# One transformer layer on one core: one written order for first stage, attention and output projection

## The chip, the cores and the metric

The kernel runs on one core of one Trainium2 chip. The metric is device time in microseconds (us), the median of three runs. A core has TensorE (PE, with its weight loads as PEld), VectorE (DVE), ScalarE (ACT), GpSimd (POOL) and SyncE (SP), which runs the DMA queue of the weights. SBUF is the on-chip memory, PSUM the banks into which TensorE sums.

## The reference

One encoder layer with 256 tokens, width D = 2048, 32 query heads and 8 key/value heads of 64, and an MLP of width 8192. A vector c modulates it: six rows of 2048 values scale, shift and gate.

```python
mod = silu(c) @ mod_w + mod_b                       # 2048 x 12288
sh_m, sc_m, g_m, sh_f, sc_f, g_f = split(mod, 6)
h = x * (1 + sc_m) + sh_m
q, k, v = split(h @ w_qkv + b_qkv)                  # 2048, 512, 512 columns
q, k = rope(q), rope(k)
s = mask(q @ k.T / 8)                               # |q - k| <= 128
p = softmax with a learned sink logit per head (s)
x = layer_norm(alpha * x + (1 + g_m) * ((p @ v) @ w_o + b_o))
h = x * (1 + sc_f) + sh_f
u = square(relu(h @ w1 + b1))
out = layer_norm(alpha * x + (1 + g_f) * (u @ w2 + b2))
```

## The kernel before

**Products.** Tokens come in two tiles of 128. A product in fp32 is done as three products of split numbers (mm3, L684 to L687): high part with high part (L685), high with the low part of the weight (L686), low with high (L687). Weights come in chunks of 1 MB, 128 x 2048 numbers, on the queue of SyncE (L335) into a ring of raw buffers: 5 of them, and 3 more (raws2) in the first stage. ScalarE casts each half of a chunk to its high part wh (L382, L393), VectorE subtracts that from the raw numbers and gets the low part wl (L351). The rings of wh and wl have 5 buffers each. A chunk of the first stage is 24 matmuls with 512 moving columns.

**Modulation.** mod_w is 96 chunks of 1 MB. Each is either taken by TensorE or by VectorE. On TensorE (Mod.quad, L455 to L463) four matmuls with 32 columns each stand side by side in the array; a chunk is 32 recorded matmuls of 128 columns or 16 of 256. On VectorE (Col.step, L498) it is one multiply with sum over 128 x 2048 numbers, with the row silu(c) spread over all partitions in cb. MIXP, FFP and GMP say who takes which: of 16 column tiles for the first scale and shift, 10 go to TensorE (two chunks each), of the gate of the mixer 8 chunks, of the MLP's scale and shift 16; together 44 chunks on TensorE and 52 on VectorE. Before the end of the output projection VectorE takes 28 of its.

**First stage.** x is transposed and modulated tile by tile, and each modulated tile can be multiplied with the columns of w_qkv. "Units" are chunks that hold four (tile, column block) pairs, "quarters" are chunks of four tiles by one column block. A planner, first_order (L80), lists the operations of this stage on the three engines with costs and due times for 17 chunks (SEQ); the code emits them in that order, and keep_in_program_order, through S.pinned (L342), makes each engine keep it.

**Attention and output projection** (scores from 165.1 us on, the last projection matmul at 349.16). A loop over n writes them in steps: scores of 4 heads for one token tile (L922), softmax, transposes of the probabilities (L964), the product with the values (L980), and between them a late chunk of w_qkv or a chunk (c, j) of w_o, where c is a block of 512 output columns and j one of four groups of 8 heads. There the Tile framework sets the order on each engine, with a few added order-only dependencies. The output of chunk (c, j) is summed in SBUF: VectorE adds each part to ys (L1075 for j = 0 with the bias, L1077 for j = 1 and 2). After j = 2, project_0 (L1084) multiplies by the gate and adds alpha times x (L1088, L1089). After j = 3, add_gated (L986) does the gate product, the addition to x and the LayerNorm statistics (L989, L990, L991).

**Behind the projection.** When the last block has its statistics, norm_scalars (L1002) computes mean and inverse deviation on VectorE (with one square root on ScalarE), normed applies them: for the first token tile on VectorE (L1032), for the second on ScalarE (nmr at L1027, applied at L1030). Then TensorE transposes the tile (L1167), ScalarE or VectorE modulates it (L1173, L1179), and the first MLP product with the chunks w1a begins (L1238). At the same time pump (L356) emits casts, low parts and modulation of the chunks that come next; of the MLP's modulation four chunks for TensorE are planned just behind the first chunk of w1a (plan_late(4)), and W1_FILL spreads the rest between the chunks of w1a.

Of the kernel before, what the change touches and what calls it, by code (L numbers as in the profile page):

```python
# [66 lines left out]
SEQ = [(0, [1, 2]), (1, [3]), (2, []), ((0, 3), [4]), ((0, 4), [5]), (3, [6]), (4, [7]), (5, []), ((1, 3), [8]), ((1, 4), [9]), (6, [10]), (7, [11]), (8, [12]), ((2, 3), [13]), (9, [14]), (10, [15]), (11, [])]  # L67
# [3 lines left out]
def first_loads():  # L71

    out = [("m", 0, 0), ("m", 0, 1)]
    for n, ks in SEQ:
        out.append(("w", n))
        out += [("m", k, i) for k in ks for i in range(2)]
    return out


def first_order():  # L80

    cost = dict(gP=1.1, gD=2.37, r=.27, c=.3, a=.16, H=.55, T=.42, S=.42, h=1.0, l=1.18, u=1.37, e=.6, sp=.85, cp=.6)
    ops = {}

    def op(key, eng, after, rank, kind=None):
        ops[key] = eng, cost[kind or key[0]], after, rank

    for k in range(NK):
        g0, g1 = ("g", k, 0), ("g", k, 1)
        if MIXP[k]:  # L90
            op(g0, "PE", [("m", k, 0)], 0, "gP")
            op(g1, "PE", [("m", k, 1), g0], 0, "gP")
            op(("r", k), "ACT", [g1], 0)
            op(("c", k), "PE", [("r", k)], 0)
            op(("a", k), "DVE", [("c", k)], 0)
        else:
            for i, g in enumerate((g0, g1)):
                op(g, "DVE", [("m", k, i), ("cp", 3)], 2, "gD")
# [4 lines left out]

    halves, last, freed = [], {"e": [("cp", 3)]}, []
    for n, _ in SEQ:
        q = type(n) is tuple
        for x in range(2):
            h, l = ("h", n, x), ("l", n, x)
            op(h, "ACT", [("w", n)] + [("h",) + v for v in halves[-1:]], 1)
            op(l, "DVE", [h] + [("l",) + v for v in halves[-1:]], 1)  # L110
# [5 lines left out]
            freed.append(("u", n, 2 + x if q else 2 * x + 1))  # L116
        for i in range(4):
            ks = range(4 * n[0], 4 * n[0] + 4) if q else [UNITS[4 * n + i][0]]
            after = [("l", n, i % 2 if q else i // 2)] + [("S", k) for k in ks] + last.get(q, [])
            if q and i % 2 == 0:  # L120
                after += last.get("e", [])
            op(("u", n, i), "PE", after, 3)
            last[q] = [("u", n, i)]
# [11 lines left out]
    while ops:
        while len(land) < len(loads) and slots:
            v = loads[len(land)]
            d = 2.47 * (1 + XK.get(v[1], 0) / 4 * (v[0] == "m" and v[2] == 0 and v[1] > 0))
            at = max(at, slots.pop(0) + 2.6) + d
            land[v] = at + .1  # L140
        best = None
        for key, (eng, d, after, rank) in ops.items():
            t = engine[eng]
            for x in after:
                if x in done:
                    e, end = done[x]
                    t = max(t, end + (0 if e == eng else .35 if e == "PE" else .15))
                elif x in land:
                    t = max(t, land[x])
                else:  # L150
                    break
            else:
                if best is None or (round(t, 2), rank, ranks[key]) < best[0]:
                    best = (round(t, 2), rank, ranks[key]), key, t
# [1335 lines left out]
```

## Time and profile before

| | |
|---|---|
| three runs | 1086.92, 1085.59, 1086.79 us; median 1086.79 |
| span of the profiled execution | 1083.7 us, 3.1 less than the median |
| last column-tile modulation matmul of the first stage | 132.1 us |
| first and last scores matmul | 165.1, 311.1 us |
| last matmul of the output projection | 349.16 us |
| first matmul of the MLP | 356.10 us |
| modulation chunks on TensorE, on VectorE | 44, 52 |

The profile is that of one execution. The span runs from its first to its last recorded instruction; the time of a run holds some microseconds around it, and no separate time is given for the profiled execution. A row of a timeline has the start in us, the length from the first start to the last end of what it holds, engine, source line, operation, tiles (out<-in), and the count; in brackets the idle time before and what ended it. Matmuls overlap one another, so the distance of two starts says what one takes, not its length.

### The profile page before, as it was taken

Reading aid. Unit: us, or ns where it says so; the run is one execution under the profiler, and the core shown is the slowest. Engines: PE = TensorE matmul, PEld = TensorE weight load, DVE = VectorE, ACT = ScalarE, POOL = GpSimd, SP = SyncE. Lnnn points to the kernel's source line nnn. Section 1 sums busy time; section 2 is a strip of 40 time slices with the busy share of each in tenths; the row PEclk is TensorE's granted clock in tenths of the full one; section 3 lists DMA queues with packets and bytes.
Section 4 is the critical chain, followed back from the end, with each engine's and each line's share of the span. In section 5 each row is a group of like instructions: output and inputs, shape, how many; then the busy total and the mean of one; then the engine's idle time right before and its main releaser. Section 6 shows DMA issues by size and latency. Waiting matters only on the chain.

```text
span 1083.7 us, 16256 instructions
## 1 busy us (share of the span) xinstructions
PE 1064.7 (98%) x6519; PEld 881.5 (81%) x6519; DVE 785.3 (72%) x1134; ACT 527.5 (49%) x814; POOL 19.7 (2%) x41
## 2 busy tenths in 40 slices
PE   8999999999999999999999999999999999999997
PEld 6777776677777899988888888888888888888885
DVE  3587689798799888754688789656665557665795
ACT  2453348777772646633345443344553334554340
POOL 2000000000000000000000010000000000000000
PEclk9999999999999999999999999999999999999999
DMA  9999997898973997555777889756555555557522
GB/s 380 425 425 425 427 407 270 352 348 344 391 277 122 420 352 273 193 194 194 272 272 274 295 293 319 297 203 222 194 194 188 192 193 201 181 181 263 194 78 78
DMA packets 43692, 292.75 MB, mean 270 GB/s; under 512 B 4916, under 2 KB 5076, under 8 KB 9824
## 3 DMA queue, kind: packets, MB, share of 16 engines
q1 hardware_dynamic: 40256, 281.82, 69.3%
q0 software_dynamic: 2496, 8.43, 2.3%
q10 hardware_dynamic: 864, 1.45, 0.4%
q8 instruction: 51, 0.84, 0.3%
q14 instruction: 25, 0.20, 0.0%
HBM read 289.57 MB, written 2.11 MB: 269 GB/s over the span
## 4 chain that ended last, share of the span: by engine, by line
PE 91%; DVE 5%; DMA 1%; ACT 1%; issue 1%; SPq 0%; DVEq 0%; ACTq 0%
PE pa L685 17%; PE pa L687 17%; PE pa L686 16%; PE pa L1264 16%; PE pa L1266 8%; PE pa L1240 3%; PE pa L1238 3%; PE pa L1239 3%; DVE raw L498 2%; PE pm L458 2%; PE gv L458 1%; PE pa L922 1%; PE pt L964 1%; PE pa L980 1%; DMA raw<-in_mod 1%; DVE wl L351 1%
## 5 line engine op out<-in xcount | busy, mean ns | idle before, releaser
L351 DVE TENSOR_TENSOR wl<-raw,wh 128x1024 fp32r<-128x1024 f32 x332 | 403.7, 1222 | 222.4 <-ACT wh L382 205.6
L382 ACT CAST wh<-raw 128x1024 fp32r<-128x1024 f32 x298 | 311.6, 1052 | 346.3 <-PE pa L687 203.1
L685 PE MATMUL pa<-wh,g 128*128 128x512 f32 x816 | 324.1, 398 | 2.7 <-ACT g L782 1.4
L687 PE MATMUL pa<-wh,g 128*128 128x512 f32 x816 | 319.3, 391 | 0.5 <-DVE g L984 0.4
L686 PE MATMUL pa<-wl,g 128*128 128x512 f32 x816 | 319.0, 391 | 0.5 <-DVE wl L351 0.4
L1264 PE MATMUL pa<-g,wh 128*128 128x512 f32 x768 | 192.3, 392 | 0.0
L685 PEld LDWEIGHTS pa<-wh,g 128*128 128x128 f32 x816 | 153.3, 188 | 42.7 <-issue 8.2
L687 PEld LDWEIGHTS pa<-wh,g 128*128 128x128 f32 x816 | 153.3, 188 | 34.6 <-issue 1.3
L686 PEld LDWEIGHTS pa<-wl,g 128*128 128x128 f32 x816 | 153.5, 188 | 31.4 <-DVE wl L351 1.2
L1264 PEld LDWEIGHTS pa<-g,wh 128*128 128x128 f32 x768 | 138.3, 189 | 25.1 <-ACT wh L382 0.2
L498 DVE CUSTOM_DVE_ANT_0 raw<-raw,cb 128x2048 f32<-128x2048 f32 x52 | 118.5, 2283 | 9.3 <-ACT cb L868 5.6
L1266 PEld LDWEIGHTS pa<-g,wl 128*128 128x128 f32 x768 | 104.8, 190 | 7.5
L1266 PE MATMUL pa<-g,wl 128*128 128x256 f32 x768 | 107.1, 282 | 0.0
L1240 PE MATMUL pa<-g,wl 128*128 128x256 f32 x256 | 72.3, 284 | 1.9 <-DVE wl L351 1.9
L1238 PE MATMUL pa<-g,wh 128*128 128x256 f32 x256 | 72.7, 285 | 0.3 <-ACT g L1173 0.3
L1239 PE MATMUL pa<-g,wh 128*128 128x256 f32 x256 | 72.4, 284 | 0.0
L1240 PEld LDWEIGHTS pa<-g,wl 128*128 128x128 f32 x256 | 48.9, 192 | 2.1 <-DVE wl L351 2.1
L1238 PEld LDWEIGHTS pa<-g,wh 128*128 128x128 f32 x256 | 49.1, 192 | 1.0 <-ACT g L1173 0.6
L1239 PEld LDWEIGHTS pa<-g,wh 128*128 128x128 f32 x256 | 49.1, 192 | 0.4 <-issue 0.4
L393 ACT CAST wh<-raw 128x1024 fp32r<-128x1024 f32 x34 | 34.8, 1048 | 21.8 <-DMA raw<-in_wqkv 19.6
L939 ACT ACTIVATE g<-g,nm 128x256 f32<-128x256 f32 x64 | 31.8, 498 | 13.1 <-DVE nm L929 13.0
L929 DVE CUSTOM_DVE_ANT_0 g<-pa,msk,nsnk 128x256 f32<-128x256 f32 x64 | 27.1, 477 | 6.3 <-PE pa L922 6.3
(204 smaller groups left out, 743.6 us busy)
## 6 DMA issues: line engine op xcount, KB each, us to landing
raw<-in_mod SPq DMA_DIRECT2D x96, 1024.0 KB, 8.8
raw<-in_w SPq DMA_DIRECT2D x64, 1024.0 KB, 4.8
raw<-in_w1b SPq DMA_DIRECT2D x48, 1024.0 KB, 4.8
raw<-in_wqkv SPq DMA_DIRECT2D x24, 1024.0 KB, 15.3
raw<-in_wo SPq DMA_DIRECT2D x16, 1024.0 KB, 7.4
raw<-in_w1a SPq DMA_DIRECT2D x16, 1024.0 KB, 7.4
g<-in_x SPq DMA_DIRECT2D x4, 512.0 KB, 9.1
gb<-in_lnrow POOLq DMA_DIRECT2D x8, 256.0 KB, 5.7
```

The costliest lines, as they stand in the source:

```text
L351: self.pinned(nc.vector.tensor_sub(l, r, f32(self.hs[n])))
L382: self.last[n] = nc.scalar.copy(h, s)
L393: self.pinned(nc.scalar.copy(h, s))
L498: S.pinned(nc.vector.tensor_tensor_reduce(out=raw, in0=raw, in1=cb, scale=1.0, scalar=0.0, op0=OP.mult, op1=OP.add, accum_out=self.dst))
L685: S.pinned(nc.tensor.matmul(ps, xh, wh, start=start, stop=False))
L686: nc.tensor.matmul(ps, xh, wl, start=False, stop=False)
L687: S.prev = nc.tensor.matmul(ps, xl, wh, start=False, stop=stop).ins
L1238: nc.tensor.matmul(o, wh(w, 128), hh, start=new, stop=False)
L1239: nc.tensor.matmul(o, wh(w, 128), hl, start=False, stop=False)
L1240: nc.tensor.matmul(o, wl(w, 128), hh, start=False, stop=end)
L1264: nc.tensor.matmul(ps, wh(k, 128), ff_in(k), start=k == 0, stop=False)
L1266: nc.tensor.matmul(ps[:, :256], wl(k, 128), ff_in(k)[:, :256], start=False, stop=k == NK - 1)
```

## The change

The diff does these things together.

1. One planner, flow_order, lists the operations of first stage, attention and output projection, on TensorE, VectorE and ScalarE, from the load order FLOW. The code emits them by `for key in KEYS`, and P() ties each instruction to the one before it on its engine with an order-only dependency. FLOW has 21 weight chunks before the last tile of the first stage (12 units and 9 quarters) where SEQ had 17.
2. Modulation: MIXP gives TensorE 9 of 16 tiles (10 before), GMP gives it 12 of 16 chunks of the gate, now 128 wide (8 before, 256 wide), FFP gives it none of the MLP's 32 (16 before). TensorE has 30 chunks, VectorE 66.
3. The output projection stays in PSUM: out_of[c] holds the two banks of a column block for all four j. The bias comes by one matmul per block and token tile (bias_rows) instead of a broadcast that VectorE adds. The sums at L1075 and L1077 and project_0 go; the addition to x takes alpha with it.
4. The scores' loops change places: the half of the array's rows (s) is now the outer one, the pair of heads in it (i) the inner one.
5. The last chunk, (2, 2) in FLOW, is done by project_last behind the plan. There `before` is empty, so that P(), and S.pinned with it, sets no order; S.pinned called keep_in_program_order before.
6. W1_FILL plans 8 modulation chunks of the MLP between the chunks of w1a, all for VectorE, and plan_late(4) goes.

```diff
-MIXP = tuple(int(k not in (4, 6, 8, 10, 12, 14)) for k in range(16))
+MIXP = tuple(int(k not in (6, 7, 9, 11, 12, 13, 15)) for k in range(16))
-FFP = (2, 2, 4, 0)
-GMP = 1
+FFP = (0, 0, 0, 0)
+GMP = 3
...
+    "m", 0, 1, "m", "m", "m", 2, (0, 5), (0, 3), 3, "m", "m", "m", (0, 4), 4, "m", (1, 4), 5, (1, 5), "m", 6, "m",
...
+    ("o", 3, 3), "f", ("o", 2, 3), "f", ("o", 2, 2), "f", "f", "f", "f", "f",
...
+    def P(i):
+        if before:
+            e = i.ins.engine
+            if before.get(e):
+                tc.add_manual_dep(i.ins, before[e], ORDER_ONLY, reason="order")
+            before[e] = i.ins.name
+        return i
...
         def pinned(self, i):
 
             if self.pin:
-                tc.keep_in_program_order(i)
+                P(i)
...
-    W1_FILL = [1, 1, 1, 0, 1, 1, 1, 3, 0, 0, 0, 0, 0, 0, 0, 0]
+    W1_FILL = [0, 1, 1, 1, 1, 1, 1, 1, 1, 0, 0, 0, 0, 0, 0, 0]
     S.plan(a["w1a"][W1A[0]])
-    plan_late(4)
...
-        for i in range(2):
-            c = (2 * rp + i) * 256 + t * 128
             for s in range(2):
-                h = slice(64 * s, 64 * s + 64)
-                nc.tensor.matmul(pss[s][:, i * 256:i * 256 + 256], qT[j][h, c:c + 128],
-                                 kT[h, j * 256:j * 256 + 256], start=True, stop=True)
+                for i in range(2):
+                    c = (2 * self.rp + i) * 256 + self.t * 128
+                    h = slice(64 * s, 64 * s + 64)
+                    P(nc.tensor.matmul(self.pss[s][:, i * 256:i * 256 + 256], qT[h, c:c + 128],
+                                       kT[h, self.j * 256:self.j * 256 + 256], start=True, stop=True))
...
-            if j == 0:
-                nc.vector.tensor_add(y, ps, bo(c))
-            elif j < 3:
-                nc.vector.tensor_add(y, y, ps)
-            else:
-                add_gated(ps, t, c, g1, st)
-        if j == 2:
-            project_0(c)
...
+    def project(wh, wl, c, j, t, rs):
+
+        if c not in out_of:
+            out_of[c] = banks(), [0] * NT
+        pss, begun = out_of[c]
+        oh, ol = oT[j]
+        for r in rs:
+            s = slice(t * 512 + r * 128, t * 512 + r * 128 + 128)
+            begun[t] += 1
+            mm3(pss[t], oh[:, s], ol[:, s], wh(r), wl(r), begun[t] == 1, begun[t] == 16)
+
+    def project_last(c, j):
+
         wh, wl = S.main()
...
+            project(wh, wl, c, j, t, range(4))
+            if t:
+                S.done(False)
+                S.done(False)
+                S.stop, S.behind, S.pin = 0, False, True
+                S.nh, S.nl = 2, 0
+                S.pump(4)
+            add_gated(out_of[c][0][t], t, c, g1, st, ALPHA)
+            sc.append(norm_scalars(st[t]))
+            normed(0, t)
+        S.nl = 2
+        S.pump(0, 2 * S.im + 2)
...
+    for key in KEYS:
+        op, *v = key
...
+    S.pin = S.deep = False
+    before.clear()
     S.pace = VECS
     S.behind = True
-    for n in range(OUT_AT + 16):
...
+    ff_columns(0)
+    project_last(*last_wo)
```

The next rows are VectorE's own order in the kernel before, from the second token tile's last gate product (L989) to its nmr (L1027).

```order
L989 TENSOR_TENSOR tmp<-pa,g_2793 128x512
L1015 SCALAR_TENSOR_TENSOR qq<-r_3439,ve 128x1
L990 TENSOR_TENSOR g_2304<-g_2304,tmp 128x512
L1016 TENSOR_SCALAR qq<-qq 128x1
L991 BN_STATS st_2803<-g_2304 128x6
L1017 TENSOR_TENSOR r_3439<-r_3439,qq 128x1
L1005 BN_AGGR mv<-st_2803 128x2
L1032 TENSOR_SCALAR g_2298<-g_2298,mv,r_3439 128x512
L1007 TENSOR_SCALAR ve<-mv 128x1
L1013 RECIPROCAL r_3512<-sd 128x1
```

After these come the last scalars up to nmr, and no other work stands between them. In the changed kernel the piece ahead of the second tile's product (the second L1093) reads so; L655 is a sum of the modulation (two rows each), L1093, L1097 and L1098 are product, addition and statistics:

```order
L655 ISA raw,modf<-raw,cb 128x2048
L655 ISA modf 128x1
L1093 TENSOR_TENSOR tmp<-pa,g_3008 128x512
L655 ISA raw,modf<-raw,cb 128x2048
L655 ISA modf 128x1
L1097 SCALAR_TENSOR_TENSOR g_2773<-g_2773,tmp 128x512
L1093 TENSOR_TENSOR tmp<-pa,g_3008 128x512
L1098 BN_STATS st_213<-g_2773 128x6
L1097 SCALAR_TENSOR_TENSOR g_2773<-g_2773,tmp 128x512
L1112 BN_AGGR mv<-st_213 128x2
L509 TENSOR_TENSOR wl<-raw,wh 128x1024
L1114 TENSOR_SCALAR ve<-mv 128x1
```

One sum of the modulation stands between the two products, two more of them directly ahead of the first row, and the first low part (L509) is already in the chain. The end of the same chain in the changed kernel, up to nmr (L1134):

```order
L509 TENSOR_TENSOR wl<-raw,wh 128x1024
L1139 TENSOR_SCALAR g_2769<-g_2769,mv,r_3386 128x512
L1122 SCALAR_TENSOR_TENSOR qq<-r_3422,ve 128x1
L509 TENSOR_TENSOR wl<-raw,wh 128x1024
L1123 TENSOR_SCALAR qq<-qq 128x1
L655 ISA raw,modf<-raw,cb 128x2048
L655 ISA modf 128x1
L1124 TENSOR_TENSOR r_3422<-r_3422,qq 128x1
L1181 TENSOR_TENSOR b_125<-b_125,modf 128x4
L655 ISA raw,modf<-raw,cb 128x2048
L655 ISA modf 128x1
L1134 SCALAR_TENSOR_TENSOR nmr<-mv,r_3422 128x1
```

Between these two pieces stand two more low parts and one more sum, so the chain from the second product to nmr holds five low parts and three sums. On TensorE the end of the output projection read so before (pt are the transposes behind the LayerNorm, L1238 the first MLP products):

```order
L685 MATMUL pa<-wh,g_3115 128x512
L686 MATMUL pa<-wl,g_3115 128x512
L687 MATMUL pa<-wh,g_3116 128x512
L458 MATMUL pm<-raw,cact 32x256 x32
L1167 MATMUL pt<-ident,g_2298 128x128 x8
L1238 MATMUL pa<-g_3527,wh 128x256
L458 MATMUL pm<-raw,cact 32x256 x8
L1238 MATMUL pa<-g_3527,wh 128x256
```

and reads so now:

```order
L842 MATMUL pa<-wh,g_2579 128x512
L843 MATMUL pa<-wl,g_2579 128x512
L844 MATMUL pa<-wh,g_2580 128x512
L1323 MATMUL pt<-ident,g_2769 128x128 x8
L1394 MATMUL pa<-g_3435,wh 128x256 x2
L1395 MATMUL pa<-g_3435,wh 128x256
L1396 MATMUL pa<-g_3435,wl 128x256
```

The four modulation chunks behind the last projection matmul and the one behind the first MLP matmul are gone (L458, 8 written matmuls each), and the transposes follow directly.

More of the change, by code (lines that the diff above doesn't have):

```diff
@@ L68 @@
-XK = {0: 2, 2: 2, 4: 4, 8: 4, 12: 4}
[L71 to L76, printed above, removed]
-    return out
[L80 to L86, printed above, removed]
+FLOW = [
[6 rows of a table added]
+]
+XK = {0: 2, 2: 2, 4: 4, 8: 4, 12: 4}
@@ L115, in first_order @@
             halves.append((n, x))
-            freed.append(("u", n, 2 + x if q else 2 * x + 1))
+        if n == weights[-1]:
+            break
         for i in range(4):
[L118 to L123, printed above, removed]
@@ L134, in first_order @@
-    ranks = {k: i for i, k in enumerate(ops)}
[L135 to L140, printed above, removed]
-        best = None
[L142 to L149, printed above, removed]
-                else:
[L151 to L154, printed above, removed]
-        _, key, t = best
-        eng, d, _, _ = ops.pop(key)
-        engine[eng] = t + d
-        done[key] = eng, t + d
+            after = [("l", n, i % 2 if kind == "q" else i // 2)] + last.get(kind == "u", [])
@@ new lines, in flow_order, with over @@
+    ranks = {k: i for i, k in enumerate(ops)}
+    wait, then = {}, {}
+    for key, v in ops.items():
+        wait[key] = len(v[2])
+        for x in v[2]:
+            assert x in ops or x in have, x
+            then.setdefault(x, []).append(key)
+    at, begin, ready, out = 4.6, dict.fromkeys(ops, 0.0), [k for k in ops if not wait[k]], []
+    engine, used, back, slots, nl, tiled = dict(PE=0.0, ACT=0.0, DVE=0.0, Q=0.0), {}, [0.0] * 8, [0.0] * (RAWS + MORE), 0, False
+    def over(key, end, eng=None):
+        for k in then.get(key, ()):
+            begin[k] = max(begin[k], end + (0 if eng in (None, ops[k][0]) else AFTER[eng]))
+            wait[k] -= 1
+            if not wait[k]:
+                ready.append(k)
@@ new lines, in flow_order @@
+    while ready or len(out) < len(ops):
+        while nl < len(loads) and (slots or loads[nl][0] == "x"):
+            v = loads[nl]
+            if v[0] == "x":
+                at += 5.0
+            else:
+                at = max(at, slots.pop(0) + 2.6) + 2.47 * (1 + XK.get(v[1], 0) / 4 * (v[0] == "m" and v[2] == 0 < v[1]))
+            over(v, at + .1)
+            nl += 1
+        best = None
+        for key in ready:
+            eng, kind, _, rank, banks, _, _ = ops[key]
+            if banks and (used.get(banks[0], 0) + len(banks) > BANKS[banks[0]] or len(banks) > len(back)):
+                continue
+            t = max([engine[eng], begin[key]] + back[len(banks) - 1:len(banks)] * bool(banks))
+            v = (round(t + LATER.get(kind, 0), 2), rank, ranks[key])
+            if best is None or v < best[0]:
+                best = v, key, t
+        assert best, ("nothing can go on", ready)
+        _, key, t = best
+        ready.remove(key)
+        eng, kind, _, _, banks, frees, slot = ops[key]
+        end = t + COST[kind]
+        if eng == "PE":
+            now = kind in ("gP", "sc", "va")
+            end += LEAVE * (tiled and not now)
+            tiled = now
+        engine[eng] = end
+        for b in banks:
+            used[b] = used.get(b, 0) + 1
+            back.pop(0)
+        for b in frees:
+            used[b] -= 1
+            back.append(end + .2)
+            back.sort()
+        if slot:
+            slots.append(end)
+        over(key, end, eng)
@@ new lines, in hybrid_kernel @@
+    load_x(0)
+    split_bias, bq = bias_rows(a["bqkv"], QKV)
+    split_bo, bo = bias_rows(a["bo"], D)
+    msk = masks()
+    for _ in rotary_tables():
+        pass
+    S.pin = True
+    before[None] = None
+    idle(12)
+    S.loads()
+    st = [sml.tile([128, 4, 6], F32, name=f"st{t}", bufs=2) for t in range(NT)]
+    chunk_of = {}
+    for v in LOADS:
+        if v[0] == "w":
+            chunk_of[v[1]] = len(chunk_of)
+    first_late = max(i for i, v in enumerate(LOADS) if v[0] == "m")
@@ new lines, in hybrid_kernel, with product, bias, row_bias @@
+    soon = {v[1] for v in LOADS[:first_late] if v[0] == "w"}
+    def product(n, i):
+        w = S.halves(chunk_of[n])
+        if type(n) is int:
+            unit(*w, n, i)
+        elif n[0] == "o":
+            project(*w, n[1], n[2], i % 2, (i // 2 * 2, i // 2 * 2 + 1))
+        elif n in soon:
+            quarter(*w, *n, i)
+        else:
+            late(*w, *n, i)
+    def bias(p):
+        for t in range(NT):
+            bq((sums[p] if p < 3 else late_of[p])[t], CORD[p])
+    def row_bias(c):
+        for t in range(NT):
+            bo(out_of[c][0][t], c, False)
```

782 lines of the change are left out of this document (415 added, 367 removed), and 4 rows, old and new, of the table FLOW.

## The prediction

> **What bounds the kernel now.** I read the page first: the span, the busy times and the chain that ended last.
>
> ```profile
> span 1083.7 us, 16256 instructions
> ...
> PE 1064.7 (98%) x6519; PEld 881.5 (81%) x6519; DVE 785.3 (72%) x1134; ACT 527.5 (49%) x814; POOL 19.7 (2%) x41
> ...
> PE 91%; DVE 5%; DMA 1%; ACT 1%; issue 1%; SPq 0%; DVEq 0%; ACTq 0%
> ```
>
> TensorE is busy for 1064.7 of 1083.7 us, so waits can give back 19 us in all; more must come from work taken off it. The second view gives the busy time by stretch (columns: stretch, its length, then PE, PEld, DVE, ACT, POOL busy with counts, granted clock, DMA share, GB/s).
>
> ```profile
> 13.10:16.50 3.40, 1.56 (x34) 1.33 (x35) 2.70 (x3) 1.77 (x3) 0.00 (x0) 0.99 0.98 411
> 16.50:19.90 3.40, 3.40 (x36) 2.37 (x35) 0.00 (x0) 0.00 (x0) 0.00 (x0) 0.50 1.05 432
> 19.90:160.00 140.10, 135.54 (x1075) 106.04 (x1066) 99.78 (x130) 59.30 (x81) 0.00 (x0) 1.00 1.01 425
> 160.00:325.00 165.00, 164.25 (x1196) 119.18 (x1195) 143.81 (x307) 122.91 (x297) 3.78 (x7) 1.00 0.87 329
> 325.00:349.40 24.40, 24.40 (x116) 19.18 (x114) 22.12 (x37) 4.96 (x6) 0.00 (x0) 1.00 0.38 130
> 349.40:356.10 6.70, 4.98 (x73) 2.81 (x73) 6.02 (x18) 3.72 (x7) 0.00 (x0) 1.00 0.68 249
> 356.10:460.00 103.90, 101.97 (x846) 99.61 (x847) 85.61 (x116) 63.92 (x95) 0.00 (x0) 1.00 0.82 308
> ```
>
> From 19.9 to 349.4 us, the part that the change rewrites, TensorE idles 4.56 + 0.75 + 0 = 5.3 us, and full DMA (share 1.01) stands only over the first 140 us. The third view is TensorE's timeline around the end of the output projection, which I call T0: the last projection matmul starts at 349.16. Such matmuls follow one another in 0.22 to 0.23 us (348.94 to 349.16), so T0, when the next could start, is 349.39 (columns: start, us from the first start of a row to its last end, engine, line, operation, tiles, shape, count [idle time before, releaser]).
>
> ```profile
> 348.94 0.39 PE L686 MATMUL pa<-wl,g 128*128 128x512 f32 x1
> 349.16 0.39 PE L687 MATMUL pa<-wh,g 128*128 128x512 f32 x1
> 349.48 3.66 PE L458 MATMUL pm<-raw,cact 128*32 128x256 f32 x64
> 353.07 0.44 PE L1167 MATMUL pt<-ident,g 128*128 128x128 f32 x2
> 354.90 0.87 PE L1167 MATMUL pt<-ident,g 128*128 128x128 f32 x6 [1.39 <-ACT g L1030]
> 356.10 0.39 PE L1238 MATMUL pa<-g,wh 128*128 128x256 f32 x1 [0.33 <-ACT g L1173]
> 356.42 1.07 PE L458 MATMUL pm<-raw,cact 128*32 128x256 f32 x16
> ```
>
> After T0 nothing of the MLP can start before gate, residual and LayerNorm are through. Before, TensorE fills that wait with four modulation chunks (64 matmuls, 3.66 us) and loses little. The same place in the timelines of VectorE and ScalarE:
>
> ```profile
> 349.85 0.67 DVE L989 TENSOR_TENSOR tmp<-pa,g 128x512 f32<-128x512 f32 x1
> ...
> 353.84 0.16 DVE L1027 SCALAR_TENSOR_TENSOR nmr<-mv,r 128x1 f32<-128x1 f32 x1
> 353.92 2.35 DVE L351 TENSOR_TENSOR wl<-raw,wh 128x1024 fp32r<-128x1024 f32 x2
> 354.03 0.81 ACT L1030 ACTIVATE g<-g,nmr,r 128x512 f32<-128x512 f32 x1 [1.06 <-DVE nmr L1027]
> ```
>
> The second token tile's gate product starts 0.46 us after T0, the last LayerNorm scalar (nmr) stands 4.0 us later, and only after it come the first lo halves (wl, two in 2.35 us). ScalarE applies nmr, and 2.1 us after 354.0 the first MLP matmul runs. This chain, not TensorE's work, sets 349.4 to 356.1.
>
> **The change, part by part.** All sums go against the profiled span, 1083.7 us; the median of the shown runs, 1086.79, lies 3.1 above it, and I add that at the end. Prices of the modulation, in groups by line and shape (operation, tiles, count | busy us, mean ns of one | idle time before, releaser):
>
> ```profile
> L498 DVE CUSTOM_DVE_ANT_0 raw<-raw,cb 128x2048 f32<-128x2048 f32 x28 | 63.7, 2283 | 6.1 <-ACT cb L868 5.6 <-DMA raw<-in_mod 0.5
> ...
> L458 PE MATMUL gv<-raw,cact 128*32 128x128 f32 x640 | 22.3, 282 | 2.8 <-DMA raw<-in_mod 2.8
> ...
> L458 PE MATMUL pm<-raw,cact 128*32 128x256 f32 x160 | 10.7, 385 | 0.0
> ...
> L458 PE MATMUL pm<-raw,cact 128*32 128x128 f32 x256 | 8.6, 276 | 0.0
> ```
>
> These rows hold everything before T0: 20 chunks of 32 matmuls (gv), 10 of 16 that are 256 wide, 8 of 32 that are 128 wide. Timelines of TensorE around one such chunk and around two score groups give what a chunk and a switch take:
>
> ```profile
> 295.88 0.39 PE L687 MATMUL pa<-wh,g 128*128 128x512 f32 x1
> 296.19 1.08 PE L458 MATMUL pm<-raw,cact 128*32 128x128 f32 x32
> 297.20 0.50 PE L687 MATMUL pa<-wh,g 128*128 128x512 f32 x1
> 297.54 0.40 PE L685 MATMUL pa<-wh,g 128*128 128x512 f32 x1
> ```
>
> ```profile
> 290.83 1.13 PE L922 MATMUL pa<-g,g 64*128 64x256 f32 x8
> 291.89 0.50 PE L685 MATMUL pa<-wh,g 128*128 128x512 f32 x1
> ...
> 299.69 0.49 PE L922 MATMUL pa<-g,g 64*128 64x256 f32 x2
> ```
>
> A. TensorE modulation before T0. The ten 256-wide chunks go (1.00 us each: 356.42 to the next matmul at 357.42 is one of them), two gv chunks go and four 128-wide ones come (1.01 us each, 296.19 to 297.20): -10.0 - 2.0 + 4.0 = **-8.0 us**, all on the bounding engine.
>
> B. Going into and out of the four-column form costs 0.31 - 0.23 ahead of a chunk and 0.34 - 0.23 behind it, 0.19 us. In the written orders eight such places fewer stand: **-1.5 us**, between -1.5 and 0 where a neighbour hides it.
>
> C. The output bias goes from VectorE to eight matmuls of 0.23 us: **+1.8 us**.
>
> D. Scores. A group of 8 recorded matmuls takes 1.06 us (290.83 to 291.89): neighbours work on different 64-row halves, two begin together (the pair at 299.69), so the group is two slots of 0.53. The new order puts two of the same half behind one another. If it then takes three slots, each of 16 groups costs 0.53 more, 8.5 in all; if the hardware pairs as before, 0. I take the middle, about 0.25 a group, **+4 us**, since no row shows this order. [...]
>
> E. Stalls of TensorE before T0. VectorE gets 11 more modulation sums before T0 (39 in the new order against these 28): 25.1 us; it loses 32 sums of output parts, priced at the 0.67 us of the product at 349.85: -21.4. Together 3.7 us on an engine busy for 99.78 + 143.81 + 22.12 = 265.7 of 329.5 us; on the mean there is room. More weight chunks (21 instead of 17) move into the DMA-bound part, where TensorE waited most. Bounds: -5.3, if all idle goes, to +10, if the idle share of the first stage (4.56 of 140.1, 3.3%) held over some 305 us of the rewritten part. I take **0**: added sums and removed waits both touch the same slack.
>
> T0 thus moves by -8.0 - 1.5 + 1.8 + 4 + 0 = -3.7 us.
>
> F. The bubble behind T0. In the new order VectorE has five lo halves and three modulation sums between the second tile's gate product and nmr, in a chain that had nothing between its steps. By the two lo halves at 353.92 (2.35, so 1.18 each) and the row of L498 (2.28) that is 5 x 1.18 + 3 x 2.28 = 12.7 us. It hides behind nothing: TensorE's four fillers are gone, and its next instruction behind the last projection matmul is the transpose that waits for this LayerNorm. One more sum stands between the first tile's product and the second's, three ahead of both. The first tile's sum ends about 2.8 us ahead of T0 (12 matmuls of 0.23); if VectorE is free there, product, sum and addition (0.6 + 2.28 + 0.6) put the second tile's product at T0 + 1.1, 0.7 later than now. If all four sums come late, 9.1 later. I take 3 us: **+15.7**, between 13.4 and 21.8. The lo halves done there aren't done later, but the 1.9 us of idle time in 356.1 to 460 shows that they were not waited for.
>
> G. Two more chunks stood between the first MLP matmuls in the old order. The one at 356.42 I take as cover for waits that remain, the other as its 1.0 us and a switch of 0.2 on the path: **-1.2 us**, between -2.4 and 0.
>
> H. Clock. The stretch 13.1 to 16.5 has 1.84 us of idle time, and the next 3.4 us run at 0.50. A bubble of some 20 us should do the same: half of 3.4, **+1.7 us** (0 to 3.4). [...]
>
> J. The stage after it (356.1 to 460) has the same number of modulation sums, 8, placed a little differently: between -1.9 (its idle time) and +2.4 (one more sum ahead of a lo half that is waited for); I take **0**.
>
> Sum: -3.7 + 15.7 - 1.2 + 1.7 + 0 = +12.5, so a span of 1096.2 and a time of **1099.3 us**.
>
> **The rivals.**
>
> 1. VectorE comes late to the chain, and TensorE starves ahead of it. For: VectorE is busy for 22.12 of 24.40 us just ahead of T0 and for 143.81 of 165 before. Against: over the whole it has slack, and four TensorE chunks' casts are gone. Lag 9.1 in place of 3 (+6.1) and E at +6: about 1111.4.
>
> 2. Scores need three slots in every group: D is 8.5, 1103.8. For: the same 64 rows of the array are asked for twice in succession. Against: only the pairs' starts are seen, not a conflict. [...]
>
> 3. The other side: faster. T0 comes earlier by more than the bubble costs. With A, B and C in full, D at 0 and all 5.3 us of idle time gone, T0 moves by -13.0; the bubble at its least is 12.7 + 0.7 - 1.2 - 1.9 = +10.3 with no half clock. Together -2.7: 1084.1. It decides from the point where T0 comes 10.3 us earlier at the smallest bubble, 16.2 at the one that I took (15.7 - 1.2 + 1.7). For: the new order is one plan over stages that were planned apart. Against: the idle time that it could remove is 5.3 us by the windows.
>
> **How the numbers follow.** My forecast has 0.48, rival 1 0.20, rival 2 0.16, rival 3 0.16. Of rival 3 I give 0.10 to faster by over 0.2% and 0.06 to within it (0.2%, 2.2 us, is about what a measurement of this kernel can tell from no change: 1084.6 to 1089.0). All others are slower: 0.84. The time is the forecast's, 1099.3. The range reaches from 1086, in the middle of rival 3's, to 1113, a little beyond rival 1's; what it leaves out is the faster part of rival 3 (about 0.1) and rival 1 with rival 2 on top (under 0.1).
>
> **What would show it.** In the profile after: 18 to 22 us between the last projection matmul and the first MLP matmul, where there were 6.9 (349.16 to 356.10); lo halves and modulation sums of VectorE inside the LayerNorm chain there; a granted clock near 0.5 just behind; the last projection matmul near 345.5; 30 chunks of modulation on TensorE; score groups between 1.06 and 1.6 us. I am wrong if the bubble is below 13 us, since then VectorE reached those lo halves ahead of the chain or in its gaps, or if T0 comes before 335, since then the idle time that I read isn't what the plan removes.

## The result and the profile after

The changed kernel takes 1102.14 us (median of 4 runs, 1101.69 to 1103.28) where the kernel before takes 1086.19 (1085.48 to 1086.92): ratio 1.0147, 95% interval 1.0132 to 1.0161. The forecast was 1099.3 in a range of 1086 to 1113.

The page of the changed kernel, with the same three lines as before:

```profile
span 1100.3 us, 15899 instructions
...
PE 1055.6 (96%) x6330; PEld 884.8 (80%) x6330; DVE 798.6 (73%) x1131; ACT 528.1 (48%) x813; POOL 22.3 (2%) x45
...
PE 86%; DVE 9%; DMA 3%; ACT 1%; issue 1%; SPq 0%; DVEq 0%; POOLq 0%
```

TensorE has 9.1 us less work (1055.6 against 1064.7) and the span is 16.6 us longer: its idle time went from 19 to 45 us. In the chain that ended last VectorE's share went from 5% to 9%. Where that is, a cut of both kernels at T0 and at the first MLP matmul shows; the kernel before first, then the changed one (columns as before):

```profile
0.00:349.40 349.40, 339.70 (x2532) 255.56 (x2532) 272.81 (x497) 191.92 (x392) 9.97 (x25) 1.00 0.89 356
356.10:1083.70 727.60, 720.07 (x3915) 623.08 (x3915) 506.46 (x621) 331.87 (x416) 9.74 (x16) 1.00 0.64 229
```

```profile
0.00:343.40 343.40, 332.09 (x2442) 258.21 (x2442) 278.46 (x488) 193.68 (x394) 11.46 (x27) 0.99 0.92 369
343.40:372.00 28.60, 2.40 (x9) 1.43 (x8) 26.65 (x44) 4.71 (x7) 1.05 (x2) 0.57 0.77 294
372.00:1100.30 728.30, 721.06 (x3881) 625.20 (x3880) 493.51 (x600) 329.76 (x412) 9.76 (x16) 0.99 0.62 215
```

T0 came 6.0 us earlier (343.43 against 349.39), the wait behind it grew from 6.7 to 28.6 us, and the rest is 0.7 longer: -6.0 + 21.9 + 0.7 = 16.6. In the wait TensorE is busy for 2.4 us, VectorE for 26.7. TensorE's timeline there, from the last projection matmul to the first MLP matmul:

```profile
343.20 0.39 PE L844 MATMUL pa<-wh,g 128*128 128x512 f32 x1
363.67 0.69 PE L1323 MATMUL pt<-ident,g 128*128 128x128 f32 x2 [20.08 <-DVE g L1139]
370.48 1.54 PE L1323 MATMUL pt<-ident,g 128*128 128x128 f32 x6 [6.12 <-ACT g L1137]
372.04 0.80 PE L1394 MATMUL pa<-g,wh 128*128 128x256 f32 x2
```

The transposes wait 20.08 us for the first token tile's normalisation on VectorE and 6.12 for the second's. VectorE's timeline says what it did meanwhile (L655 is a modulation sum, L1093 a gate product, L509 a lo half, L1134 nmr):

```profile
343.18 2.27 DVE L655 CUSTOM_DVE_ANT_0 raw<-raw,cb 128x2048 f32<-128x2048 f32 x1
...
349.80 0.68 DVE L1093 TENSOR_TENSOR tmp<-pa,g 128x512 f32<-128x512 f32 x1
350.40 2.28 DVE L655 CUSTOM_DVE_ANT_0 raw<-raw,cb 128x2048 f32<-128x2048 f32 x1
...
353.22 0.68 DVE L1093 TENSOR_TENSOR tmp<-pa,g 128x512 f32<-128x512 f32 x1
...
355.18 1.16 DVE L509 TENSOR_TENSOR wl<-raw,wh 128x1024 fp32r<-128x1024 f32 x1
...
369.42 0.15 DVE L1134 SCALAR_TENSOR_TENSOR nmr<-mv,r 128x1 f32<-128x1 f32 x1
```

The first gate product could have started some 2.5 us ahead of T0, when its sum was complete (its last matmul started at 340.48); it starts 6.4 behind it, after three modulation sums. The second starts 9.8 us behind T0 (0.46 before), and nmr stands 16.2 us after that (4.0 before). By groups, VectorE did this between 343.2 and 369.45:

```profile
L655 DVE CUSTOM_DVE_ANT_0 raw<-raw,cb 128x2048 f32<-128x2048 f32 x7 | 15.8, 2279 | 0.0
L509 DVE TENSOR_TENSOR wl<-raw,wh 128x1024 fp32r<-128x1024 f32 x5 | 5.9, 1187 | 0.0
```

Seven sums and five lo halves (low parts), 21.7 us, and the wait grew by 21.9. That the two are so near is partly chance: by the starts it is 9.3 us more lag, 12.2 more chain and 0.4 more behind nmr, and in the lag are also 1.2 us of the first tile's product and addition, which lay ahead of T0 before. What happened ahead of T0 is in the stretches that answer to those of before:

```profile
13.10:16.50 3.40, 0.00 (x0) 0.00 (x0) 2.65 (x9) 0.73 (x2) 0.00 (x0) 0.99 1.01 420
16.50:19.90 3.40, 2.17 (x5) 1.80 (x6) 2.78 (x8) 2.97 (x5) 0.00 (x0) 0.50 1.01 420
19.90:160.00 140.10, 140.10 (x1089) 112.92 (x1089) 105.24 (x133) 59.01 (x78) 0.00 (x0) 0.99 1.01 423
160.00:325.00 165.00, 161.30 (x1184) 121.68 (x1183) 146.85 (x307) 123.02 (x302) 1.64 (x3) 0.99 0.83 320
```

With 21 weight chunks in it, the first stage has no idle time left (4.56 us before). But in the first two stretches TensorE now idles 4.6 us (1.84 before), and 3.7 us (0.75 before) between 160 and 325. Two rows of the waits by line say for what (us in total, times, longest):

```profile
PE pa L842 <- ACT g L872: 4.8, 1, 4.8
...
PE pm L616 <- DMA raw<-in_mod: 3.0, 1, 3.0
```

The first is the first unit of w_qkv, which waits for ScalarE's part of the first modulated tile where a modulation chunk stood before; the second is a chunk of the gate whose load came late. Busy time ahead of T0 fell by 7.6 us (339.70 to 332.09), idle time grew by 1.6: that makes the 6.0.

The clock has a part in it too. In the changed kernel TensorE runs at half clock in two stretches ahead of T0, 10.2 us together, behind the start and behind the late gate chunk; before, only the 3.4 us at 16.5 did.

```profile
16.43:23.26 6.83, 5.53 (x14) 4.42 (x15) 6.17 (x12) 5.51 (x8) 0.00 (x0) 0.50 1.01 422
228.06:231.47 3.41, 3.22 (x40) 2.17 (x42) 1.56 (x2) 0.00 (x0) 0.00 (x0) 0.50 0.73 223
```

TensorE is busy at half clock for 8.75 us there, 3.4 before; half of the difference, some 2.7 us, is an estimate of what that cost.

### The profile page after: what moved, and what is told of

Its sections match the earlier page's. It is cut to its first block, busy times and chain, and to the rows that moved or that the text cites. A ratio compares the mean times of both kernels' runs of the same rounds, so it can differ in the third digit from the quotient of the medians.

```text
span 1100.3 us, 15899 instructions
## 1 busy us (share of the span) xinstructions
PE 1055.6 (96%) x6330; PEld 884.8 (80%) x6330; DVE 798.6 (73%) x1131; ACT 528.1 (48%) x813; POOL 22.3 (2%) x45
## 4 chain that ended last, share of the span: by engine, by line
PE 86%; DVE 9%; DMA 3%; ACT 1%; issue 1%; SPq 0%; DVEq 0%; POOLq 0%
PE pa L1420 16%; PE pa L842 16%; PE pa L844 15%; PE pa L843 15%; PE pa L1422 8%; DVE raw L655 3%; PE pa L1395 3%; PE pa L1396 3%; PE pa L1394 3%; DVE wl L509 2%; PE gv L616 1%; PE pa L1075 1%; DMA raw<-in_wqkv 1%; PE pt L1056 1%; PE pa L1010 1%
## 5 line engine op out<-in xcount | busy, mean ns | idle before, releaser
L509 DVE TENSOR_TENSOR wl<-raw,wh 128x1024 fp32r<-128x1024 f32 x332 | 402.9, 1222 | 224.3 <-ACT wh L540 204.7
L1420 PEld LDWEIGHTS pa<-g,wh 128*128 128x128 f32 x768 | 138.3, 189 | 25.1 <-ACT wh L540 0.2
L655 DVE CUSTOM_DVE_ANT_0 raw<-raw,cb 128x2048 f32<-128x2048 f32 x66 | 150.2, 2283 | 9.4 <-DMA raw<-in_mod 9.4
L1395 PE MATMUL pa<-g,wh 128*128 128x256 f32 x256 | 74.2, 290 | 1.6 <-DVE g L1337 1.6
L1394 PE MATMUL pa<-g,wh 128*128 128x256 f32 x256 | 74.1, 290 | 0.0
L1395 PEld LDWEIGHTS pa<-g,wh 128*128 128x128 f32 x256 | 50.6, 198 | 2.2 <-DVE g L1337 2.2
L1394 PEld LDWEIGHTS pa<-g,wh 128*128 128x128 f32 x256 | 50.6, 198 | 0.4 <-ACT g L1329 0.4
L1027 ACT ACTIVATE g<-g,nm 128x256 f32<-128x256 f32 x64 | 31.9, 505 | 0.0
L1323 PE MATMUL pt<-ident,g 128*128 128x128 f32 x32 | 5.3, 313 | 26.2 <-DVE g L1139 20.1
## 6 DMA issues: line engine op xcount, KB each, us to landing
raw<-in_wqkv SPq DMA_DIRECT2D x24, 1024.0 KB, 11.2
```

Source lines behind the costliest of these rows:

```text
L509: self.pinned(nc.vector.tensor_sub(l, r, f32(self.hs[n])))
L655: S.pinned(nc.vector.tensor_tensor_reduce(out=raw, in0=raw, in1=cb, scale=1.0, scalar=0.0, op0=OP.mult, op1=OP.add, accum_out=self.dst))
L1394: nc.tensor.matmul(o, wh(w, 128), hh, start=new, stop=False)
L1395: nc.tensor.matmul(o, wh(w, 128), hl, start=False, stop=False)
L1420: nc.tensor.matmul(ps, wh(k, 128), ff_in(k), start=k == 0, stop=False)
```

## The experiments

Theory 1: the loss is VectorE's work that the written order puts between the last projection matmul and nmr, and each instruction of it costs its own length. Rivals: the work has to be done anyway and comes back as waits behind the chain; or VectorE is late because of its backlog; or what is missing is TensorE's filler. The table holds what the traces of all runs show, worked out from the starts of four instructions: T0 (start of the last projection matmul + 0.23), the start of the second tile's gate product against T0 (lag), from there to nmr (chain), and from T0 to the first MLP matmul (wait).

| kernel | T0 | lag | chain | wait | span | median of the runs |
|---|---|---|---|---|---|---|
| before | 349.39 | 0.46 | 3.99 | 6.7 | 1083.7 | 1086.2 |
| changed | 343.43 | 9.78 | 16.21 | 28.6 | 1100.3 | 1102.1 |
| e1_pin | 340.21 | 6.93 | 9.27 | 18.8 | 1085.2 | 1090.4 |
| e2_tail | 340.09 | 4.47 | 14.52 | 21.6 | 1089.4 | 1095.7 |
| e3_fill | 342.37 | 6.97 | 10.46 | 20.0 | 1094.2 | 1097.7 |
| e4_chain_free | 340.01 | 2.76 | 3.99 | 9.0 | 1081.0 | 1088.5 |
| e5_sums_before | 350.35 | 0.40 | 18.50 | 22.2 | 1101.0 | 1102.4 |
| e6_two_sums_back | 340.43 | 1.27 | 8.29 | 12.2 | 1086.5 | 1090.4 |
| e7_chain_free_again | 341.46 | 2.78 | 3.99 | 9.4 | 1083.5 | 1087.1 |
| e8_chain_free_look | 346.59 | 2.77 | 3.99 | 9.4 | 1088.7 | (1090.5, one run) |
| e9_start_and_gate | 346.92 | 3.76 | 4.12 | 11.2 | 1090.1 | 1090.8 |
| e10_start_and_gate_b | 343.17 | 0.46 | 4.64 | 7.7 | 1080.1 | 1082.1 |

The profiled run of each of e1 to e4 was the fastest of its kernel's runs, up to 5.8 us under the median, so spans are compared with spans and medians with medians. The kernel before ran beside each group of experiments (1086.1 us with e1 to e4, 1086.0 with e5 to e8, 1086.7 with e9 and e10); the changed kernel ran once, beside the 1086.2 of the first row.

**e1: the written order kept behind the plan.**

```diff
         def pinned(self, i):
 
-            if self.pin:
+            if self.pin and before:
                 P(i)
+            elif self.pin:
+                tc.keep_in_program_order(i)
```

> The changed kernel, but casts, low parts and sums issued in project_last keep their written order again, as before the change. On VectorE the five low parts leave the LayerNorm chain, the sum between the two gate products too, and two sums stay in it; the three sums ahead of the first product stay. Theory 1 (the chain: each VectorE instruction written between the last projection matmul and nmr costs its own length): 5 x 1.18 + 2 x 2.28 = 10.4 us less than the 1102.1 us of the changed kernel, about 1091.7. Rival (given back: low parts and sums have to be done anyway, so TensorE waits for them behind the chain): only the two sums come off, about 1097.5.

1090.42 us; against the kernel before 1.0040 (1.0029 to 1.0052), so 11.7 us less than the changed kernel: theory 1, which had 10.4. VectorE's groups from T0 to nmr:

```profile
L657 DVE CUSTOM_DVE_ANT_0 raw<-raw,cb 128x2048 f32<-128x2048 f32 x5 | 11.3, 2285 | 0.0
```

No lo half is left in the chain, and they don't come back as waits: from the first MLP matmul to the end it takes 726.2 us, 2.0 less than in the changed kernel. The three sums ahead of the first product stay, and so does the lag (6.9). Three of the 9.8 us by which the wait is shorter are lag, seven are chain. T0 of this trace is 3.2 us earlier than in the changed kernel, though nothing is edited ahead of it: the time ahead of T0 differs from run to run, which e7 and e8 come back to.

**e2: the last three sums of the plan moved behind the projection.**

```diff
-    ("o", 3, 3), "f", ("o", 2, 3), "f", ("o", 2, 2), "f", "f", "f", "f", "f",
+    ("o", 3, 3), "f", ("o", 2, 3), "f", ("o", 2, 2), "f", "f",
...
-    W1_FILL = [0, 1, 1, 1, 1, 1, 1, 1, 1, 0, 0, 0, 0, 0, 0, 0]
+    W1_FILL = [0, 2, 2, 2, 1, 1, 1, 1, 1, 0, 0, 0, 0, 0, 0, 0]
```

> The changed kernel, but the last three modulation sums of the plan are loaded and done among the first chunks of w1a instead. No sum stands directly ahead of the first gate product; five low parts and two sums stay in the chain. Theory 1: first product at most 0.5 us behind T0 instead of 6.4, sum between the products gone, one sum less in the chain, 6 + 2.3 + 2.3 = 10.6 us less, about 1091.5. Rival (VectorE is late there because of its backlog, whatever stands last): 2.3 us less, about 1099.8.

1095.70 us, 1.0093 (1.0076 to 1.0110) of before: 6.4 us less than changed, between theory 1 (10.6) and the backlog (2.3). Groups from T0 to nmr:

```profile
L655 DVE CUSTOM_DVE_ANT_0 raw<-raw,cb 128x2048 f32<-128x2048 f32 x3 | 6.8, 2280 | 0.0
L509 DVE TENSOR_TENSOR wl<-raw,wh 128x1024 fp32r<-128x1024 f32 x5 | 6.0, 1194 | 0.0
```

Both were right in part. The chain is as theory 1 had it: 14.5 us = 4.0 + 5 lo halves + 2 sums (6.0 + 4.6 = 10.6). The lag fell to 4.5, not to 0.5: VectorE was still at a sum and at the gated sums of the block before, 3.9 us of backlog at T0.

**e3: TensorE's filler back, nothing else.**

```diff
-FFP = (0, 0, 0, 0)
+FFP = (0, 0, 0, 4)
```

> The changed kernel, but the last eight modulation chunks of the MLP go to TensorE (four of them behind the last projection matmul, as before the change), so that no VectorE sum is left for the window of the LayerNorm; its low parts and the three sums ahead of the first product stay. Theory 1: the sum between the products and three sums in the chain go, 9.1 us, and four of the eight TensorE chunks lie outside the wait, +4.8: 4.3 less, about 1097.8. Rival (the loss is TensorE's missing filler and its clock): the wait is covered again, about 1087.

1097.66 us, 1.0103 (1.0088 to 1.0118): 4.5 us less than changed, where theory 1 had 4.3 and the filler rival 15. With TensorE's filler and the lo halves and the plan's last sums in place the wait is still 20.0 us.

```profile
342.45 1.07 PE L616 MATMUL pm<-raw,cact 128*32 128x256 f32 x16
345.69 1.70 PE L616 MATMUL pm<-raw,cact 128*32 128x256 f32 x16 [2.17 <-DMA raw<-in_mod]
351.13 1.06 PE L616 MATMUL pm<-raw,cact 128*32 128x256 f32 x2 [3.74 <-DMA raw<-in_mod]
```

The fillers themselves waited for their loads inside the wait, at no cost, since the chain ended later.

**e4: all three together, and the fillers planned behind the first chunk of w1a.** To the edits of e1 and e3 come:

```diff
-    ("o", 3, 3), "f", ("o", 2, 3), "f", ("o", 2, 2), "f", "f", "f", "f", "f",
+    ("o", 3, 3), "f", ("o", 2, 3), "f", ("o", 2, 2), "f", "f",
...
-    W1_FILL = [0, 1, 1, 1, 1, 1, 1, 1, 1, 0, 0, 0, 0, 0, 0, 0]
+    W1_FILL = [0, 1, 1, 1, 1, 1, 1, 1, 0, 0, 0, 0, 0, 0, 0, 0]
...
+    m_ff[3].plan(4)
```

> The changed kernel with all three: the written order kept in project_last, the last three sums of the plan moved among the chunks of w1a, and the last eight MLP modulation chunks on TensorE, four of them planned behind the first chunk of w1a. The LayerNorm chain on VectorE then reads as before the change, with nothing between its steps. Theory 1: T0 keeps its 6.0 us and the wait is again 6.7 instead of 28.6: 1102.1 - 21.9 + 2.4 for the two more TensorE chunks behind T0 = about 1082.6, faster than the kernel before (1086.2). Rival (given back): the same as before or slower, 1086 to 1092.

1088.53 us, 1.0015 (1.0001 to 1.0030) of before. The chain is 3.99 us again, as before the change, and the wait looks as it did:

```profile
339.78 0.39 PE L847 MATMUL pa<-wh,g 128*128 128x512 f32 x1
340.10 3.66 PE L618 MATMUL pm<-raw,cact 128*32 128x256 f32 x64
345.65 0.44 PE L1326 MATMUL pt<-ident,g 128*128 128x128 f32 x2 [1.89 <-DVE ve L1117]
347.82 1.04 PE L1326 MATMUL pt<-ident,g 128*128 128x128 f32 x6 [1.74 <-ACT g L1140]
349.02 0.79 PE L1397 MATMUL pa<-g,wh 128*128 128x256 f32 x2 [0.16 <-ACT g L1332]
```

Of the 21.9 us 19.6 are gone (2.3 of lag, VectorE's backlog, stay). The profiled run, 1082.73 us, met the 1082.6 of theory 1; the median lies 6 us above it, on the rival's side. So the wait is explained, and something else makes the runs of this kernel differ; e7 and e8 look at that.

**e5: the same cause put into the kernel before.**

```diff
-FFP = (2, 2, 4, 0)
+FFP = (2, 2, 0, 0)
```

> The kernel before, with one number changed: the third group of the MLP's modulation (8 chunks) goes to VectorE in place of TensorE. Its LayerNorm chain then has six sums written between the first tile's normalisation and the second tile's nmr, where there was nothing, and TensorE has no filler there. Theory 1 (the sums in the chain cost their own length): 6 x 2.28 = +13.7, less four TensorE chunks that lay outside the wait (-4.0), half clock behind the wait +3: about 1086.2 + 12.7 = 1099. Rival (the wait is set by something else and the filler only used it): 1082 to 1086, since TensorE has eight chunks less.

1102.36 us, 1.0144 (1.0130 to 1.0159) of before: +16.4 by medians, where theory 1 had +12.7 and the rival none or a gain. One number makes the old kernel as slow as the changed one. The groups of its VectorE from T0 to nmr, where none stood:

```profile
L498 DVE CUSTOM_DVE_ANT_0 raw<-raw,cb 128x2048 f32<-128x2048 f32 x6 | 13.5, 2286 | 0.2 <-DMA raw<-in_mod 0.2
```

Chain 18.5 = 4.0 + 13.5 and 1.0 of small gaps. The time that I took off for TensorE's lighter work did not come: T0 is even 1.0 us later than before, and the rest takes 728.4 us against 727.6.

**e6: a dose of two sums.** The kernel of e4, with one sum less in the plan, which by the written order puts two sums into the chain:

```diff
-    ("o", 3, 3), "f", ("o", 2, 3), "f", ("o", 2, 2), "f", "f",
+    ("o", 3, 3), "f", ("o", 2, 3), "f", ("o", 2, 2), "f",
...
-    W1_FILL = [0, 1, 1, 1, 1, 1, 1, 1, 0, 0, 0, 0, 0, 0, 0, 0]
+    W1_FILL = [0, 2, 1, 1, 1, 1, 1, 1, 0, 0, 0, 0, 0, 0, 0, 0]
```

> The kernel with the free chain (e4), but one more sum of the plan's end is loaded behind the projection, which by the written order puts two sums back into the LayerNorm chain, both between the second tile's gate product and nmr. Theory 1: two lengths, 4.5 us more than the free chain in the same call, and the wait 11.2 us in place of 6.7. Rival (the time is set by what TensorE and the queue do, the wait only shifts): within 1 us of it.

1090.36 us, 3.3 more than e7, measured beside it on the same chip, where theory 1 had 4.5; against the kernel before it is 1.0034 (1.0022 to 1.0045), and e7's interval, below, ends at 1.0015. The chain grew from 3.99 to 8.29 us, by two sums less 0.2, and the lag shrank by 1.5, probably since the sum that left the plan had stood in VectorE's backlog. That is 2.8 in the wait (9.4 to 12.2).

**e7 and e8: the kernel of e4 twice more.**

> The kernel with the free chain (e4) once more, to see whether its profiled 1082.7 us or its timed median of 1088.5 us holds. Theory 1 alone gives 1082.6. If the new order of the first stage makes the time depend on the start (a wait of 4.7 us there, and half the clock behind it), the runs spread between 1082 and 1091 again, with the difference ahead of T0.

> A second look at the same kernel: T0 between 340 and 344 us, the wait behind it 6.7 us; what the time differs from the other look lies ahead of T0.

e7: 1087.10 us (1083.21 to 1089.57), 1.0005 of before (0.9994 to 1.0015). The wait is 9.0, 9.4 and 9.4 us in the three profiles of this kernel, and the rest 731.9 to 732.8; T0 is 340.01, 341.46 and 346.59. The expected wait of 6.7 us was too short (the lag stays), and the last T0 lies outside the 340 to 344 that I expected. So 6.6 of the 7.7 us by which the spans differ lie ahead of T0. In e8 TensorE's longest wait between 160 and 325 us is for a chunk of the gate:

```profile
228.99 1.94 PE L618 MATMUL pm<-raw,cact 128*32 128x128 f32 x32 [3.98 <-DMA raw<-in_mod]
```

The wait is 3.98 us (2.5 in e4), and the chunk behind it takes 1.94 us instead of 1.08. The matmuls take about twice their time until 234.46 (3.68 us instead of 1.95 for the next 16, L1078), and the mean clock from 160 to 250 is 0.96; in e4 it is 1.00. The other difference is the start, the same stretch in e4 and in e8:

```profile
13.10:20.00 6.90, 2.87 (x7) 2.30 (x8) 6.04 (x17) 3.92 (x7) 0.00 (x0) 0.80 1.02 423
```

```profile
13.10:20.00 6.90, 2.41 (x6) 1.93 (x7) 5.67 (x16) 3.80 (x7) 0.00 (x0) 0.71 1.01 418
```

The mean clock of this stretch is 0.80 in e4 and 0.71 in e8, that of the next 20 us 0.98 and 0.93: worked out from these means, the half clock behind the start lasts from some 17.3 to 20.7 in e4 and from some 16.0 to 22.8 in e8.

**e9 and e10: two load orders against these two waits.** Both are the kernel of e4 with other places in FLOW and another split of the MLP's sums between the plan and W1_FILL: e9 has one sum at the plan's end where e4 has two, as e6 had, and e10 has five. Of e10 the lines are shown:

```diff
-    "m", 0, 1, "m", "m", "m", 2, (0, 5), (0, 3), 3, "m", "m", "m", (0, 4), 4, "m", (1, 4), 5, (1, 5), "m", 6, "m",
+    "m", 0, "m", "m", 1, "m", 2, (0, 5), (0, 3), 3, "m", "m", "m", (0, 4), 4, "m", (1, 4), 5, (1, 5), "m", 6, "m",
...
-    "g", "G", (3, 3), (3, 5), ("o", 1, 0), "G", "G", "f", "f", "G", "g", ("o", 0, 0), "G", "f", "f", ("o", 1, 1),
-    ("o", 0, 1), "f", "G", "G", "f", ("o", 0, 2), "G", ("o", 1, 2), "f", "f", "f", ("o", 0, 3), "G", "f", "f", "f",
+    "g", "G", (3, 3), (3, 5), ("o", 1, 0), "G", "G", "f", "f", "G", "g", ("o", 0, 0), "G", "f", "G", "f", ("o", 1, 1),
+    ("o", 0, 1), "G", "f", "f", ("o", 0, 2), "G", ("o", 1, 2), "f", "f", "f", ("o", 0, 3), "G", "f", "f", "f",
...
-    ("o", 3, 3), "f", ("o", 2, 3), "f", ("o", 2, 2), "f", "f",
+    ("o", 3, 3), "f", ("o", 2, 3), "f", ("o", 2, 2), "f", "f", "f", "f", "f",
...
-    W1_FILL = [0, 1, 1, 1, 1, 1, 1, 1, 0, 0, 0, 0, 0, 0, 0, 0]
+    W1_FILL = [0, 0, 0, 0, 1, 1, 1, 1, 0, 0, 0, 0, 0, 0, 0, 0]
```

> The kernel with the free chain, and its load order changed at two places: three modulation tiles are loaded ahead of the second unit of w_qkv, so that TensorE has a modulation chunk in the wait of 4.7 us at 13 us, and two chunks of the gate are loaded ahead of a chunk of w_o and a sum of VectorE, for the wait of 2.3 to 4.0 us at 225 us. The chain stays free. Theory 1 with the start theory (those two waits and the half clock behind them are what lies between 1082 and 1091): waits 7 us less and the clock 2 us, a median of 1079 to 1082 with a spread under 3 us. Rival (the order is written against transfers that vary, so that other waits take their place): 1085 to 1089 with the same spread.

> The same with two modulation tiles ahead of the second unit, the two gate chunks spread between sums, and all of the last sums left in the plan. The chain stays free by the written order. Theory 1 with the start theory: 1079 to 1083. Rival: 1085 to 1089.

e10: 1082.06 us (1080.60 to 1085.53), 0.9969 of before (0.9959 to 0.9980). It beats both kernels: 4.6 us under the one before by medians, 20.1 under the changed one. e9: 1090.80 us, 1.0042 (1.0029 to 1.0055), slower than e4 and above even its rival's 1085 to 1089. The two waits that were meant shrank, at the start to 1.2 us in e9 and 0.2 in e10, at the gate to 0.4 or less. But others took their place: in both TensorE now waits 2.6 us at the start for the load of a modulation chunk, and in e9 these two are the longest:

```profile
PE pt L1326 <- DVE g L1142: 3.2, 1, 3.2
PE pt L763 <- DVE colm L754: 3.1, 1, 3.1
```

The first lies behind T0. The second is TensorE waiting for an addition to the gate's column on VectorE (L754, 290.46), which started behind a modulation sum and the low part of an attention output; T0 of e9, 346.92, is the latest of the kernels made from the changed one. With the tail of e6 its chain is 4.12 us, not 8.29: two sums stand among the gated sums of the block before instead (340.65 and 344.13), and why is not shown. And e10's gain does not come from where theory 1 put it. Its T0, 343.17, is no earlier than that of e4 and e7; against e7 its span is 3.4 us shorter, with T0 1.7 later, the wait 1.7 shorter and the rest 3.5 shorter. So its time met theory 1, but the two waits do not explain it. In the wait its lag is 0.46 us, the old value, with all five sums of the plan's end in the plan: the plan's last sum starts at 332.11, ahead of the gated sums of the block before, where in e1, with as many in the plan, three start behind those (the last is shown, e1 first):

```profile
344.32 2.29 DVE L657 CUSTOM_DVE_ANT_0 raw<-raw,cb 128x2048 f32<-128x2048 f32 x1
```

```profile
332.11 2.29 DVE L657 CUSTOM_DVE_ANT_0 raw<-raw,cb 128x2048 f32<-128x2048 f32 x1
```

It is where the sums stand that sets the lag, not how many the plan holds. That the rest is shorter may come from the three sums that e10 has moved out of it; how much of the gain each edit brings was not taken apart.

## Why the prediction was right, point by point

In the sum two misses of opposite sign met: the span grew by 16.6 us where I had 12.5, with the bubble 6.2 longer than forecast and T0 2.3 earlier. That the time came so near (1102.1 against 1099.3) is in part this balance.

**T0** came 6.0 us earlier, not 3.7. A, B and C met as a sum: busy time ahead of T0 fell by 7.6 us, against their 7.7. But that holds a piece of luck, since the 7.6 are net of D's 0.5 and of some 2.7 us for the clock ahead of T0, which I had not in the sum at all; without these TensorE's work fell by some 3 us more than I took, and which of the terms was too small is not shown. **D** was wrong. The new score groups take 1.07 us, as the old ones did; the row of one and of its successor:

```profile
171.20 1.14 PE L1010 MATMUL pa<-g,g 64*128 64x256 f32 x8
172.27 0.50 PE L842 MATMUL pa<-wh,g 128*128 128x512 f32 x1
```

All sixteen lie at 1.07 except two, of 1.32 and 1.26, together 0.5 us more than before. Rival 2 is out: with two neighbours of one half the group takes 1.07 us, so they made no third slot. What the two that begin together are, the rows don't say; that they are the two halves I had read into the order. **E** was +1.6 in place of 0, but as a balance: the first stage's 4.56 us of idle time went, as its plan promised, and 2.8 at the start and 3.0 for a late chunk of the gate came.

**F**, the bubble, carried the forecast: +15.7 predicted, +21.9 measured. The step that was mis-sized is the lag. I had three sums ahead of the products and one between them in view, bounded their lateness by 0.7 and 9.1 us, and took 3; it was 9.3, a little over the upper bound, because the gated sums of the block before (its gate products, additions and statistics) kept VectorE until 343.18, 0.25 us ahead of T0, and all four modulation sums came behind them. That is half of rival 1; its other half, TensorE starving ahead of T0, did not happen. The chain itself was right: 12.2 us more against 12.7. The last 0.35 us (nmr to first MLP matmul 2.61 against 2.26) goes with the transposes at half clock, six in 1.54 us against 0.87.

**G, H and J** were near as a sum: +0.7 us measured for all behind the first MLP matmul, 0.5 predicted. H was the wrong size: the clock stayed at 0.50 until about 381.6, 9.6 us into the MLP, as the three pieces of that stretch show:

```profile
372.00:378.00 6.00, 4.39 (x18) 3.78 (x18) 5.95 (x11) 4.58 (x8) 0.00 (x0) 0.50 0.50 171
378.00:381.50 3.50, 3.50 (x18) 3.50 (x18) 0.06 (x1) 0.91 (x1) 0.00 (x0) 0.50 0.52 218
381.50:390.00 8.50, 8.50 (x73) 8.50 (x72) 7.84 (x11) 5.09 (x9) 0.00 (x0) 0.99 0.65 249
```

36 matmuls at some 0.21 us instead of 0.12 cost about 3.3 us, twice what I took. TensorE's last wait in it ends here:

```profile
376.07 0.58 PE L1395 MATMUL pa<-g,wh 128*128 128x256 f32 x1 [1.35 <-DVE g L1337]
```

From there TensorE ran without a gap, and the full clock came back some 5.5 us later. I had taken one stretch of 3.4 us at half clock, as the kernel before has it at its start (16.5 to 19.9), as if it began with the first MLP matmul and no wait came in it; what brings the full clock back is not shown.

**Rival 3** needed T0 to come 10 to 16 us earlier; it came 6. e4 and e10 show that the rest of the change was worth having: with the chain free it is even with the kernel before, and with another load order faster. What is not settled is why T0 differs by up to 6.6 us between runs of one kernel; three traces put it at the start and at one late load, and no run varied these by themselves. Behind the start the clock fell in all three (0.80 in e4, 0.82 in e7, 0.71 in e8 over 13.1 to 20), behind the late load in e8 alone (0.96 over 160 to 250, 1.00 in e4 and e7). The T0 of the changed kernel is that of one trace, too.

## What to carry to other kernels

When work moves from the busy engine to one with slack, look where it lands: at a place where the first engine waits for the second, each instruction written into that chain costs about its whole length, here 21.7 us of VectorE work for a wait that grew by 21.9. A plan that stops one step ahead of such a chain can fill the place, because it does not know the chain's end; and when ordering is done by a helper, look what still calls it after it is switched off. And the written order tells the length of such a wait well (chain 12.2 against 12.7), but not when the engine arrives at it (lag 9.3 against 3): that needs its backlog at that moment.

## What the runs showed of the hardware that I had not expected

After the wait of 28.6 us TensorE ran at half clock for 9.6 us more, through 36 matmuls, the last 5.5 us of them without a gap. In the clock records of the kernel before and of the changed one every stretch at half clock, but the one that the kernel's end cuts off, lasts a whole number of times 3.41 us: 3.41 before, 6.83, 3.41 and 34.13 in the changed kernel. A single wait of 2.97 us (ended at 228.25 in the changed kernel) or 3.98 us (e8) was enough to double the modulation chunk behind it (1.93 and 1.94 us against 1.08); a wait of 2.5 us at the same place in e4 was not (clock 1.00 from 160 to 250). But in e10 TensorE idles only 1.83 us in all from 160 to 250, and the clock there is 0.98, so the length of a wait alone does not decide it. And the order of the 64-row halves in a score group made no difference: 1.07 us and 1.06.
